# Products of gate and second-norm modulation chunks held back until the next weight chunk's low halves are in VectorE's program

## The chip, the cores and the metric

The kernel runs on one core of one Trainium2 chip. Its time is the device time of one execution in microseconds (us); lower is better. The core's engines run side by side, each through an instruction list of its own: TensorE (PE: matmuls, with PEld for its weight loads), VectorE (DVE), ScalarE (ACT), GpSimd (POOL) and SyncE (SP, which issues most of the transfers). Semaphores order them against each other.

## The reference, cut to what matters

One layer of a decoder for 256 tokens of width 2048. Attention (16 heads of sparse attention and 8 of retention) and an expert stage are each wrapped in a norm with modulation in front and a gated residual add behind:

```python
c_act = jax.nn.silu(c)
mod = (c_act @ w_ada[l] + b_ada[l]).reshape(B, 6, 1, D)
shift1, scale1, gate1, shift2, scale2, gate2 = jnp.moveaxis(mod, 1, 0)
h = rmsnorm(x, g_norm_mix[l]) * (1.0 + scale1) + shift1
q_a, k_c, ..., g_r = split_cols(h @ w_in[l], IN_SIZES)
...
x = x + gate1 * (jnp.concatenate([o_nsa, o_ret], axis=-1) @ w_out[l])
h2 = rmsnorm(x, g_norm_ffn[l]) * (1.0 + scale2) + shift2
x = x + gate2 * peer_ffn(h2, peer_w_q[l], peer_sub_keys[l], peer_u[l], peer_v[l])
```

The change touches the computation of `mod`: six vectors of 2048, each a product of a 2048 x 2048 part of `w_ada` with one vector.

## The kernel before

**Two stages.** Up to about 545 us come the modulation, the first norm, the input projection, both kinds of attention and the output projection (`woutN`). The expert stage follows, up to the end at 1855 us. Weights are read once, in chunks of 128 partitions x 2048 floats (1 MB).

**A weight chunk.** `load` issues its transfer on SP's queue into a tile `raw`; there are four such slots in the first stage. `split_to` makes two parts of it, each in two column halves: ScalarE rounds it to a high part `whi` (L157), and VectorE subtracts that from it to leave a low part `wlo` (L158). There are two slots of each. TensorE then does three products for each block (activation high x weight high, high x low, low x high), so that a chunk of the output projection is 24 matmuls of 512 columns (L453). The 16 chunks of `woutN` make four tiles of 512 output columns (q = 0 to 3, four chunks each, chunks 0 to 15). Behind each tile VectorE multiplies the sums by the row of gate1 (`xg`, L719) and adds the result to the residual `xT` (L720).

**A modulation chunk.** The modulation weights are 96 more chunks of the same size, `adaT[j, k]`: j is one of the six vectors, k one of 16 pieces of it. Each uses one of the same four raw slots. VectorE multiplies it by the row of silu(c) and sums along the row into one column of `modc` (L198, in place). It is named the product here. It frees the slot, and the next transfer into that slot waits on SP's queue for it, as it waits elsewhere for a low half (L158). The chunks are taken from the list `todo` in the order j = 1 and 0 mixed, then 2, 4, 3, and six of 5; `background(pace)` takes as many as the table `PACE` says after each weight chunk. The rest of j = 5 follows in the expert stage.

**The gate row.** When the last j = 2 chunk is done, TensorE transposes that column block of `modc` (psg1, L203), ScalarE copies it out (`row2t`, L204), GpSimd's queue stores it (L205) and loads it again as a 1 MB tile with the row in every partition (`g1`, L210). The `xg` multiplications read `g1`.

**Order.** A scheduler sets each engine's instruction order from the program order and priorities. `tc.keep_in_program_order` keeps an instruction at its place in the program. The retention heads run between the chunks of the last projection tiles; their scores are `scr` (L646, L647), which read query and key blocks that VectorE puts into `xT` (L430).

Of the kernel before, what the change touches and what calls it, by code (L numbers as in the profile page):

```python
# [17 lines left out]
OP = mybir.AluOpType  # L18
# [5 lines left out]
KB = D // P  # L24
# [7 lines left out]
LATE = 6  # L32
# [83 lines left out]
def body(ctx, tc, a, out, dbg=None, stop=None):  # L116
    nc = tc.nc
# [28 lines left out]
    def load(src):  # L146
        r = raw_tile()
        i = nc.sync.dma_start(r, src)
        if ring:
            tc.keep_in_program_order(i)  # L150
        return r

    def split_to(r, hi, lo, parts=1):
        n = hi.shape[-1] // parts
        for i in range(parts):
            sl = slice(i * n, i * n + n)
            nc.scalar.copy(hi[:, sl], r[:, sl])  # L157
            nc.vector.tensor_sub(lo[:, sl], r[:, sl], hi[:, sl].bitcast(F32))  # L158

    def split(r, n=2048, parts=2):  # L160
        hi, lo = chunk_tile("whi", F32R)[:, 0:n], chunk_tile("wlo", F32R)[:, 0:n]
        split_to(r[:, 0:n], hi, lo, parts)
        return hi, lo
# [8 lines left out]
    b_col = cols[:, 0:96].rearrange("p (j k) -> p j k", k=KB)  # L172
    g_mix, g_ffn = cols[:, 96:112], cols[:, 112:128]
# [3 lines left out]
    modc = base.tile([P, 6, KB], F32, name="modc")  # L177
    scol = base.tile([P, 2, KB], F32, name="scol")
    def c_row(pool, psum=None, dst=None):

        r = pool.tile([P, D], F32, name="crow") if dst is None else dst
        if psum is None:
            nc.sync.dma_start(r, bass.AP(tensor=a["c"].tensor, offset=a["c"].offset, ap=[[0, P], [1, D]]))
            nc.scalar.activation(r, r, AF.Silu)
            return r
        c1 = raw_tile()[0:1, :]
        nc.sync.dma_start(c1, a["c"])
        for q in range(4):
            sl = slice(q * 512, (q + 1) * 512)
            ps = psum.tile([P, 512], F32, name="psc_", tag="A")  # L190
            nc.tensor.matmul(ps, ones[0:1, :], c1[:, sl], start=True, stop=True)
            nc.scalar.activation(r[:, sl], ps, AF.Silu)
        return r

    def ada_chunk(j, k, crow):

        r = load(a["adaT"][j, k])
        nc.vector.scalar_tensor_tensor(r, r, 1.0, crow, op0=OP.mult, op1=OP.mult, accum_out=modc[:, j, k:k + 1])  # L198

    def gate_store(j, ps, ident, t):  # L200

        row = dram.tile([1, D], F32, name=f"row{j}")
        nc.tensor.transpose(ps, modc[:, j, :], ident)  # L203
        nc.scalar.copy(t, ps)  # L204
        nc.gpsimd.dma_start(row.rearrange("o (k p) -> (o k) p", p=P), t)  # L205
        return row

    def row_load(dst, row):

        nc.gpsimd.dma_start(dst, bass.AP(tensor=row.tensor, offset=row.offset, ap=[[0, P], [1, D]]))  # L210
# [30 lines left out]
    def t_block(pool, src_chunk, tag="A", **kw):  # L241
        return t_blocks(pool, [src_chunk], (tag,), **kw)[0]

    def summed(ps, dst, n=S):

        nc.scalar.copy(dst, ps[:, 1, 0:n])
        nc.vector.tensor_add(dst, dst, ps[:, 0, 0:n])
# [31 lines left out]
    with ExitStack() as fctx:  # L279
# [32 lines left out]
        crow = c_row(fp, pp)  # L312
# [15 lines left out]
        def background(n=1):  # L328
            credit[0] += PACE[n] if isinstance(n, str) else n
            n = int(credit[0] + 1e-6)  # L330
            credit[0] -= n
            for _ in range(n):
                if not todo:
                    return
                j, k = todo.pop(0)
                ada_chunk(j, k, crow)
                if j == 0:
                    nc.vector.tensor_add(modc[:, 0:2, k], modc[:, 0:2, k], b_col[:, 0:2, k])
                    nc.vector.tensor_scalar(scol[:, 0, k:k + 1], modc[:, 1, k:k + 1], 1.0, g_mix[:, k:k + 1],
                                            op0=OP.add, op1=OP.mult)  # L340
                elif 1 < j < 5 and k == KB - 1:
                    nc.vector.tensor_add(modc[:, j, :], modc[:, j, :], b_col[:, j, :])
                    if j == 4:
                        nc.vector.scalar_tensor_tensor(scol[:, 1, :], modc[:, 4, :], 1.0, g_ffn, op0=OP.add, op1=OP.mult)

        def win_row(src, k, n):
            r = raw_tile()
# [14 lines left out]
        def row_in(k):  # L362
            while len(todo) > 80 + LATE - 2 * (k + 1):
                background(1)
            modulate(k, k + 1, xT[:, k:k + 1, :], 0, 0, hh, hl)

        def wait_in(dst, bk):
            for i, b in enumerate(bk):
                if i % 2:
                    nc.vector.tensor_copy(dst[:, 2 * i:2 * i + 2, :], b)  # L370
                else:
                    nc.scalar.copy(dst[:, 2 * i:2 * i + 2, :], b)

        background(2)
        bk = banks("bkA", [P, 2, S], "AASSTTOO")
        for k in range(KH):
# [66 lines left out]
        def n_tile(i, src="winN", tag="A", pace="tile"):  # L443
            ps = [pp.tile([P, 512], F32, name="psN", tag=tag) for _ in range(2)]
            for c in range(4):
                hi, lo = split(load(a[src][i, c].rearrange("p k e -> p (k e)")))
                for kk in range(4):
                    k = 4 * c + kk
                    w = slice(kk * 512, (kk + 1) * 512)
                    for tt in range(2):  # L450
                        ts_ = slice(tt * P, (tt + 1) * P)
                        for j, (x, y) in enumerate(((hh, hi), (hh, lo), (hl, hi))):
                            nc.tensor.matmul(ps[tt], x[:, k, ts_], y[:, w], start=k == 0 and j == 0,  # L453
                                             stop=k == KB - 1 and j == 2)
                background(pace)
            return ps
# [19 lines left out]
        for kv in range(2):  # L476
# [9 lines left out]
            for pb in range(16):  # L486
                i = nc.tensor.matmul(psc, w1[:, pb * P:(pb + 1) * P], blk[:, pb], start=pb == 0, stop=pb == 15)
# [34 lines left out]
        for gp in range(2):  # L522
# [3 lines left out]
            for r in range(4):  # L526
# [5 lines left out]
                for hf in range(2):  # L532
# [5 lines left out]
                    for br in range(2):  # L538
# [6 lines left out]
                        for tt, sl in ((0, slice(0, 128)), (1, slice(128, 384))):  # L545
# [3 lines left out]
                                                 accum_out=den[:, hf, tt, br:br + 1])  # L549
# [14 lines left out]
                f = lambda x: x.rearrange("p a b c d -> p (a b c) d")  # L564
# [140 lines left out]
        for q in range(4):  # L705
            sl = slice(q * 512, (q + 1) * 512)
            ps = n_tile(q, "woutN", "AS"[q % 2], "out")
            if q == 0:
                while any(j == 2 for j, _ in todo):
                    background(1)  # L710
                g1 = fp.tile([P, D], F32, name="g1", tag="cT")
                row_load(g1, gate_store(2, pp.tile([P, P], F32, name="psg1", tag="T")[0:KB, :], ident,
                                        fp.tile([KB, P], F32, name="row2t")))
            if q == 3:
                background(len(todo))
            with tc.high_priority(offset=100 if q == 3 else 0):
                for tt in range(2):
                    t = fp.tile([P, 512], F32, name="xg", tag="tmp2", bufs=3)
                    nc.vector.tensor_mul(t, ps[tt], g1[:, sl])  # L719
                    nc.vector.tensor_add(x2[:, tt, sl], x2[:, tt, sl], t)  # L720
                    sq = fp.tile([P, 512], F32, name="sq2", tag="tmp2", bufs=3)
                    nc.scalar.activation(sq, x2[:, tt, sl], AF.Square, accum_out=ss[:, tt, q:q + 1])
                    nc.gpsimd.dma_start(x2d[:, tt, sl], x2[:, tt, sl])
# [23 lines left out]
    with ExitStack() as gctx:  # L747
# [49 lines left out]
        pin = tc.keep_in_program_order  # L797
# [76 lines left out]
        def rows_in(q):  # L874

            ps = up.tile([P, 512], F32, name="psh", tag=bank("S"))
            for i in range(4):
                nc.tensor.transpose(ps[0:NS, i * P:(i + 1) * P], xT[:, 4 * q + i, TD:S], ident)
            sl = slice(q * 512, (q + 1) * 512)
            nc.scalar.copy(h2t[0:NS, sl], ps[0:NS])  # L880
            nc.gpsimd.dma_start(h2t[NS:P, sl], h2t[0:NS, sl])
# [299 lines left out]
        crow2 = gp_.tile([P, D], F32, name="crow2", tag="X1")  # L1181
# [3 lines left out]
        for i in range(16):  # L1185
            ps = first[i] if i < 2 else t_block(up, wq(i), qbank(i), dst=early if i == 2 else None)
            q = tk.tile([P, S], F32, name="pq", bufs=3)
            summed(ps, q)
            pend.append((i, q))
            if i < KB - LATE:  # L1190
                ada_chunk(5, LATE + i, crow2)
            if 4 <= i < 8:
                rows_in(i - 4)
            if i > 1:
                scores(*pend.pop(0))
            if i == 10:
                cands(1, 0, 4)
            elif i in EARLY:
                pick(1, EARLY.index(i))
# [142 lines left out]
def build(tc, a, out, dbg=None):  # L1342
    with ExitStack() as ctx:
        body(ctx, tc, a, out, dbg)
# [17 lines left out]
```

## Time and profile before

| | us |
|---|---|
| median of 3 runs | 1858.06 (1857.24 to 1858.55) |
| profiled execution | 1856.91 |
| its span | 1855.2 |
| PE busy | 1793.1 (97%) |
| DVE busy | 1485.7 (80%) |
| ACT busy | 708.7 (38%) |
| POOL busy | 366.1 (20%) |
| products L198, 96 of 2283 ns | 219.0 |
| low halves L158, 174 of 1181 ns | 200.6 |
| high halves L157, 174 of 1018 ns | 168.5 |

The span is that of one profiled execution from its first to its last instruction. "Busy" is the time in which the engine had an instruction at work; how much of it sets the end is seen only from the waits. In the rows below, `out<-in` names what is written and read, `x2` is a count, and brackets hold the idle time ahead with what ended it.

### The profile page before, as it was taken

How to read it: one execution, taken by the hardware profiler on the slowest of the kernel's cores; microseconds unless marked ns; L12 is line 12 of the kernel's file. 1: busy time of each engine (PE TensorE's matmuls, PEld its weight loads, DVE VectorE, ACT ScalarE, POOL GpSimd, SP SyncE). 2: the span in 40 equal slices, each digit the busy share in tenths (PEclk: the TensorE clock that was granted, in tenths of full speed). 3: DMA queues.
4: the chain of work that ended last, by engine and by line, in shares of the span. 5: the costliest groups of instructions: out<-in, count | busy, mean ns of one | idle time of the engine just before them, and what ended most of it. 6: DMA issues, size and time to landing. Idle time of an engine off the chain costs nothing.

```text
span 1855.2 us, 28510 instructions
## 1 busy us (share of the span) xinstructions
PE 1793.1 (97%) x11264; PEld 1571.5 (85%) x11264; DVE 1485.7 (80%) x2336; ACT 708.7 (38%) x1284; POOL 366.1 (20%) x259
## 2 busy tenths in 40 slices
PE   5899999999889999999999999999999999999997
PEld 4899878797767899999997777779999998777775
DVE  7988889889779999586498999983555558998878
ACT  3444453745435421021045555541111114555554
POOL 1000001011010012211124434420111114544210
PEclk9999899999999999999999999999999999999999
DMA  8989887889887799999889999989999989999992
GB/s 341 409 320 362 313 308 292 342 302 334 318 338 279 278 322 364 424 366 376 332 346 386 423 420 416 409 355 425 367 345 359 354 316 404 426 421 403 388 316 99
DMA packets 94616, 653.96 MB, mean 353 GB/s; under 512 B 11409, under 2 KB 11633, under 8 KB 18449
## 3 DMA queue, kind: packets, MB, share of 16 engines
q1 hardware_dynamic: 66818, 467.78, 65.2%
q0 software_dynamic: 27664, 184.37, 25.3%
q8 instruction: 88, 1.44, 0.3%
q14 instruction: 46, 0.38, 0.1%
HBM read 644.97 MB, written 4.22 MB: 350 GB/s over the span
## 4 chain that ended last, share of the span: by engine, by line
PE 87%; DVE 7%; DMA 3%; issue 1%; ACT 1%; POOL 0%; SPq 0%; ACTq 0%; POOLq 0%; DVEq 0%
PE acc L990 31%; PE psU L1111 28%; PE psN L453 8%; PE psD L354 4%; PE psA L237 3%; PE bkB L354 2%; DMA raw<-in_adaT 2%; PE psA L238 1%; PE pg L1096 1%; DVE raw L198 1%; DVE wlo L158 1%; PE bkC L354 1%; PE bvB L406 1%; DMA raw<-in_winA 1%; PE pT L552 1%
## 5 line engine op out<-in xcount | busy, mean ns | idle before, releaser
L1111 PE MATMUL psU<-xT,raw 128*128 128x160 f32 x4096 | 569.5, 300 | 0.0
L1111 PEld LDWEIGHTS psU<-xT,raw 128*128 128x128 f32 x4096 | 558.3, 190 | 0.4
L990 PE MATMUL acc<-whi,cc 128*128 128x512 f32 x1512 | 369.1, 391 | 0.0
L990 PEld LDWEIGHTS acc<-whi,cc 128*128 128x128 f32 x1512 | 283.8, 188 | 70.0 <-issue 1.5
L967 DVE TENSOR_TENSOR wlo<-raw,whi 128x2048 fp32r<-128x2048 f32 x126 | 288.1, 2287 | 55.1 <-issue 47.4
L990 PE MATMUL acc<-wlo,cc 128*128 128x512 f32 x1008 | 254.2, 392 | 0.8 <-DVE wlo L967 0.6
L964 ACT CAST whi<-raw 128x2048 fp32r<-128x2048 f32 x126 | 240.7, 1911 | 0.5 <-DMA raw<-in_v 0.5
L198 DVE SCALAR_TENSOR_TENSOR raw<-raw,crow 128x2048 f32<-128x2048 f32 x96 | 219.0, 2283 | 19.7 <-DMA raw<-in_adaT 19.6
L157 ACT CAST whi<-raw 128x1024 fp32r<-128x1024 f32 (+1 forms) x174 | 168.5, 1018 | 167.1 <-DMA raw<-in_winA 32.4
L158 DVE TENSOR_TENSOR wlo<-raw,whi 128x1024 fp32r<-128x1024 f32 (+1 forms) x174 | 200.6, 1181 | 24.2 <-ACT whi L157 23.8
L990 PEld LDWEIGHTS acc<-wlo,cc 128*128 128x128 f32 x1008 | 161.5, 161 | 63.8 <-DVE wlo L967 3.1
L453 PE MATMUL psN<-whi,act 128*128 128x512 f32 x512 | 166.9, 402 | 1.4 <-ACT act L677 0.7
L1117 DVE TENSOR_TENSOR X<-X,ge 128x160 f32<-128x160 f32 (+19 forms) x94 | 25.8, 276 | 162.7 <-ACT ge L1116 160.5
L1113 ACT ACTIVATE X<-psU 128x160 f32<-128x160 f32 (+19 forms) x102 | 25.6, 251 | 315.6 <-PE psU L1111 299.6
L453 PEld LDWEIGHTS psN<-whi,act 128*128 128x128 f32 x512 | 95.9, 189 | 25.6 <-issue 1.7
L453 PE MATMUL psN<-wlo,act 128*128 128x512 f32 x256 | 103.3, 404 | 3.4 <-DVE wlo L158 3.4
L953 ACT CAST cc<-X 128x192 fp32r<-128x192 f32 x126 | 44.0, 352 | 148.1 <-PE acc L990 147.5
L237 PE MATMUL psA<-act,whi 128*128 128x512 f32 x240 | 87.2, 404 | 3.8 <-ACT whi L157 3.8
L806 POOL DMA_INDIRECT rows<-in_urow,sx x32 | 67.1, 2097 | 105.3 <-DVE rows L847 100.4
L806 POOL DMA_INDIRECT s<-in_urow,sx x26 | 53.9, 2072 | 120.6 <-DVE s L847 86.5
L354 PE MATMUL psD<-act,whi 128*128 128x256 f32 x384 | 75.4, 294 | 0.6 <-ACT whi L157 0.6
L969 ACT CAST cc<-cc 128x64 fp32r<-128x64 f32 x126 | 30.4, 243 | 117.2 <-DVE cc L954 117.2
(363 smaller groups left out, 2551.0 us busy)
## 6 DMA issues: line engine op xcount, KB each, us to landing
raw<-in_u SPq DMA_DIRECT2D x128, 1024.0 KB
raw<-in_v SPq DMA_DIRECT2D x128, 1024.0 KB
raw<-in_adaT SPq DMA_DIRECT2D x96, 1024.0 KB
raw<-in_winN SPq DMA_DIRECT2D x16, 1024.0 KB
raw<-in_woutN SPq DMA_DIRECT2D x16, 1024.0 KB
raw<-in_wqT SPq DMA_DIRECT2D x16, 1024.0 KB
raw<-in_winB SPq DMA_DIRECT2D x16, 832.0 KB
raw<-in_winD SPq DMA_DIRECT2D x12, 1024.0 KB
```

The costliest lines, as they stand in the source:

```text
L157: nc.scalar.copy(hi[:, sl], r[:, sl])
L158: nc.vector.tensor_sub(lo[:, sl], r[:, sl], hi[:, sl].bitcast(F32))
L198: nc.vector.scalar_tensor_tensor(r, r, 1.0, crow, op0=OP.mult, op1=OP.mult, accum_out=modc[:, j, k:k + 1])
L237: nc.tensor.matmul(p_, hi[:, sl], act[:, k], start=k == 0, stop=False, skip_group_check=True)
L354: nc.tensor.matmul(bank[:, b, :], x[:, w], y[:, k, :], start=k == k0 and n == 0 and first, stop=k == k1 - 1 and n == 2, skip_group_check=True)
L453: nc.tensor.matmul(ps[tt], x[:, k, ts_], y[:, w], start=k == 0 and j == 0, stop=k == KB - 1 and j == 2)
L806: pin(nc.gpsimd.indirect_dma_start(out=r, out_offset=None, in_=src, in_offset=bass.IndirectOffsetOnAxis(ap=o, axis=0)))
L953: inorder(nc.scalar.copy(ch, xb(j)))
L964: inorder(nc.scalar.copy(hi, r))
L967: nc.vector.tensor_sub(lo[:, i:i + n], r[:, i:i + n], hi[:, i:i + n].bitcast(F32))
L990: return nc.tensor.matmul(acc[c][0:m], x, w[:, c[1] * 512:(c[1] + 1) * 512], start=jj == 0 and n == 0, stop=jj == HALF - 1 and n == 2 - c[ ...
L1111: nc.tensor.matmul(ps, w[:, k * P:(k + 1) * P], xT[:, k, 0:TU], start=k == 0, stop=k == KB - 1)
```

## The change

`ada_chunk` now issues the transfer and returns the product as a function. For j = 0 and 1 (the first norm's shift and scale) it is called at once, as before; so it is for the chunks of j = 5 in the expert stage. For j = 2 to 5 of `background` it is put in the list `pend_ada`. `split_to` empties that list behind the low halves of the next weight chunk, with `keep_in_program_order`. A second waiting product, the gate row at q = 0 and the end of the list at q = 3 empty it through `settle` at their place, without it. The bias add of `modc` and the second norm's scale go along with the last product of their vector.

```diff
         for i in range(parts):
             sl = slice(i * n, i * n + n)
             nc.scalar.copy(hi[:, sl], r[:, sl])
             nc.vector.tensor_sub(lo[:, sl], r[:, sl], hi[:, sl].bitcast(F32))
+        while pend_ada:
+            pend_ada.pop(0)(tc.keep_in_program_order)
+
+    pend_ada = []
...
     def ada_chunk(j, k, crow):
         r = load(a["adaT"][j, k])
-        nc.vector.scalar_tensor_tensor(r, r, 1.0, crow, op0=OP.mult, op1=OP.mult, accum_out=modc[:, j, k:k + 1])
+
+        def f(pin=lambda i: i):
+            pin(nc.vector.scalar_tensor_tensor(r, r, 1.0, crow, op0=OP.mult, op1=OP.mult, accum_out=modc[:, j, k:k + 1]))
+        return f
...
-                ada_chunk(j, k, crow)
+                f = ada_chunk(j, k, crow)
                 if j == 0:
+                    f()
                     nc.vector.tensor_add(modc[:, 0:2, k], modc[:, 0:2, k], b_col[:, 0:2, k])
...
-                elif 1 < j < 5 and k == KB - 1:
-                    nc.vector.tensor_add(modc[:, j, :], modc[:, j, :], b_col[:, j, :])
-                    if j == 4:
-                        nc.vector.scalar_tensor_tensor(scol[:, 1, :], modc[:, 4, :], 1.0, g_ffn, op0=OP.add, op1=OP.mult)
+                elif j == 1:
+                    f()
+                else:
+                    settle()
+
+                    def rest(pin=lambda i: i, f=f, j=j, k=k):
+                        f(pin)
+                        if j < 5 and k == KB - 1:
+                            nc.vector.tensor_add(modc[:, j, :], modc[:, j, :], b_col[:, j, :])
+                            if j == 4:
+                                nc.vector.scalar_tensor_tensor(scol[:, 1, :], modc[:, 4, :], 1.0, g_ffn, op0=OP.add, op1=OP.mult)
+                    pend_ada.append(rest)
+
+        def settle():
+            while pend_ada:
+                pend_ada.pop(0)()
...
                 while any(j == 2 for j, _ in todo):
                     background(1)
+                settle()
...
             if q == 3:
                 background(len(todo))
+                settle()
...
-                ada_chunk(5, LATE + i, crow2)
+                ada_chunk(5, LATE + i, crow2)()
```

In the changed file the lines are shifted: the product is L204, `xg` L741, the add to `xT` L742, psg1 L210, a matmul of the output projection L473, the add before the scores L450.

Every engine's order changes between about 200 and 545 us; before and behind that it is the same. Three places follow. The numbers at the names tell tiles apart.

VectorE around chunks 5 to 7 of the output projection, before. The low halves `wlo_4480` are chunk 5, `wlo_4515` chunk 6, `wlo_4550` chunk 7; a row that writes `modc` is a product:

```order
L198 SCALAR_TENSOR_TENSOR raw_4544,modc_65<-raw_4544,crow_95 128x2048
L158 TENSOR_TENSOR wlo_4480<-raw_4477,whi_4479 128x1024 x2
L678 TENSOR_TENSOR act_70<-oT_90,act_70 128x256
L198 SCALAR_TENSOR_TENSOR raw_4625,modc_65<-raw_4625,crow_95 128x2048
L158 TENSOR_TENSOR wlo_4515<-raw_4512,whi_4514 128x1024 x2
L158 TENSOR_TENSOR wlo_4550<-raw_4547,whi_4549 128x1024
L719 TENSOR_TENSOR xg_4428<-psN_4281,g1_4420 128x512
L158 TENSOR_TENSOR wlo_4550<-raw_4547,whi_4549 128x1024
```

The same place now, with chunk 5 as `wlo_4479`, chunk 6 as `wlo_4514`, chunk 7 as `wlo_4549`:

```order
L158 TENSOR_TENSOR wlo_4479<-raw_4476,whi_4478 128x1024 x2
L204 SCALAR_TENSOR_TENSOR raw_4474,modc_65<-raw_4474,crow_95 128x2048
L741 TENSOR_TENSOR xg_4428<-psN_4280,g1_4420 128x512
L158 TENSOR_TENSOR wlo_4514<-raw_4511,whi_4513 128x1024 x2
L204 SCALAR_TENSOR_TENSOR raw_4509,modc_65<-raw_4509,crow_95 128x2048
L742 TENSOR_TENSOR xT_60<-xT_60,xg_4428 128x512
L741 TENSOR_TENSOR xg_4434<-psN_4281,g1_4420 128x512
L158 TENSOR_TENSOR wlo_4549<-raw_4546,whi_4548 128x1024
L742 TENSOR_TENSOR xT_60<-xT_60,xg_4434 128x512
L158 TENSOR_TENSOR wlo_4549<-raw_4546,whi_4548 128x1024
```

The product ahead of chunk 6 is now one that is three products earlier in the list, and the first `xg`, which reads `g1`, has moved from behind chunk 6 to ahead of it.

TensorE where chunk 5 begins, before. Chunk 3 is `whi_4390`, chunk 5 `whi_4479`; psT is a head's transpose:

```order
L516 MATMUL psT_4259<-small_79,orr_4073 128x128 x2
L203 MATMUL psg1_4421<-small_79,modc_65 16x128
L453 MATMUL psN_4281<-whi_4390,act_70 128x512
L453 MATMUL psN_4282<-whi_4390,act_70 128x512
L453 MATMUL psN_4440<-whi_4479,act_70 128x512
L453 MATMUL psN_4441<-whi_4479,act_70 128x512
L453 MATMUL psN_4281<-whi_4390,act_70 128x512
L453 MATMUL psN_4281<-wlo_4391,act_70 128x512
```

The same place now, with chunk 3 as `whi_4389`, chunk 4 as `whi_4444`, chunk 5 as `whi_4478`. Psg1 stands 20 rows of chunks 4 and 3 above the first matmul of chunk 4 that is shown here:

```order
L473 MATMUL psN_4280<-whi_4389,act_70 128x512
L473 MATMUL psN_4281<-whi_4389,act_70 128x512
L473 MATMUL psN_4281<-wlo_4390,act_70 128x512
L473 MATMUL psN_4281<-whi_4389,act_70 128x512
L473 MATMUL psN_4441<-wlo_4445,act_70 128x512
L473 MATMUL psN_4441<-whi_4444,act_70 128x512
L473 MATMUL psN_4440<-whi_4478,act_70 128x512
L473 MATMUL psN_4441<-whi_4478,act_70 128x512
```

Chunk 3 held one of the two `whi` slots until behind chunk 5 (6 of its matmuls stood among or after those of chunk 5); now it ends ahead of chunk 5, and chunk 5 takes the slot that chunk 3 leaves.

VectorE ahead of the last retention scores' query block (`xT_60<-cT_91`), before:

```order
L158 TENSOR_TENSOR wlo_4088<-raw_4085,whi_4087 128x1024
L672 TENSOR_TENSOR orr_3352<-orr_3352,sg_3560 128x256
L198 SCALAR_TENSOR_TENSOR raw_4152,modc_65<-raw_4152,crow_95 128x2048
L662 BN_AGGR bmv_3374<-bst_3373 128x2 x2
L661 BN_STATS bst_3398<-por_3394 128x6 x2
L649 TENSOR_TENSOR at_3974<-scr_3971,dec_3969 128x384
L198 SCALAR_TENSOR_TENSOR raw_4155,modc_65<-raw_4155,crow_95 128x2048
L430 TENSOR_TENSOR xT_60<-cT_91,psD_4002 128x512
```

The same place now:

```order
L158 TENSOR_TENSOR wlo_4087<-raw_4084,whi_4086 128x1024
L204 SCALAR_TENSOR_TENSOR raw_4054,modc_65<-raw_4054,crow_95 128x2048
L450 TENSOR_TENSOR xT_60<-cT_91,psD_4002 128x512
L683 TENSOR_SCALAR brs_3349<-bmv_3348 128x2
L692 TENSOR_TENSOR orr_3326<-orr_3326,sg_3559 128x256
```

Between the low halves of chunk 12 of the last input tiles (`winN`) and that add stood two products and several small steps; now one product stands there. On TensorE the scores that read it stand 13 matmuls later than before.

## Prediction

> **What bounds the kernel now.** I read the page first, then stretches of 20 us, then TensorE's waits in the stretch whose order changes, and last VectorE's, ScalarE's and GpSimd's rows around each wait.
>
> ```profile
> span 1855.2 us, 28510 instructions
> PE 1793.1 (97%) x11264; PEld 1571.5 (85%) x11264; DVE 1485.7 (80%) x2336; ACT 708.7 (38%) x1284; POOL 366.1 (20%) x259
> L198 DVE SCALAR_TENSOR_TENSOR raw<-raw,crow 128x2048 f32<-128x2048 f32 x96 | 219.0, 2283 | 19.7 <-DMA raw<-in_adaT 19.6
> ```
>
> The profiled execution took 1856.91 us: the span and 1.7 us around it. That is 1.15 us below the median of the runs. TensorE (PE) is busy in 97% of the span, so the change can win only what TensorE loses in the stretch that it reorders (about 200 to 545 us; later every engine's order is as before). A product (L198) costs 2.28 us of VectorE, and before the 96 of them VectorE stood 19.6 us waiting for their transfers. Those 19.6 us are no forecast of the gain: VectorE's idle time counts only where TensorE then waits.
>
> ```profile
> 400.00:420.00 20.00, 20.00 (x162) 19.58 (x161) 18.03 (x27) 8.87 (x15) 5.55 (x3) 1.00 0.88 312
> 420.00:440.00 20.00, 18.08 (x87) 14.61 (x87) 18.40 (x32) 9.81 (x16) 2.69 (x2) 1.00 0.97 348
> 440.00:460.00 20.00, 20.00 (x95) 16.09 (x93) 19.08 (x37) 13.32 (x19) 3.79 (x3) 1.00 0.91 351
> 460.00:480.00 20.00, 19.28 (x87) 15.20 (x87) 15.47 (x21) 8.18 (x16) 1.26 (x2) 1.00 0.85 309
> 480.00:500.00 20.00, 15.92 (x61) 12.16 (x60) 14.41 (x16) 7.23 (x10) 1.66 (x3) 0.91 0.84 303
> 500.00:520.00 20.00, 20.00 (x88) 16.05 (x87) 15.58 (x16) 9.24 (x12) 1.08 (x2) 1.00 0.82 303
> 540.00:560.00 20.00, 12.57 (x54) 8.95 (x52) 14.78 (x36) 9.60 (x27) 4.01 (x6) 0.81 0.79 295
> 200.00:420.00 220.00, 218.86 (x1411) 188.16 (x1411) 193.62 (x396) 112.94 (x250) 22.33 (x24) 0.98 0.84 314
> ```
>
> The columns are the stretch, its length, busy time of PE, PEld, DVE, ACT and POOL, granted clock, DMA share, GB/s. From 200 to 420 us TensorE misses 1.1 us in all. It misses 1.92 in 420:440, 0.72 in 460:480 and 4.08 in 480:500. What is missing from 544 us on is the passage into the second norm, where the order stays. The waits have these causes (us in total, times, longest):
>
> ```profile
> PE psN L453 <- DVE wlo L158: 3.4, 1, 3.4
> PE scr L646 <- DVE xT L430: 1.9, 1, 1.9
> PE psN L453 <- ACT act L677: 0.7, 1, 0.7
> PE psN L453 <- ACT whi L157: 0.7, 1, 0.7
> 482.00:484.00 2.00, 1.33 (x6) 0.69 (x5) 0.00 (x0) 1.50 (x2) 0.00 (x0) 1.00 0.84 348
> 484.00:487.75 3.75, 0.33 (x3) 0.00 (x1) 3.50 (x4) 2.38 (x3) 0.00 (x0) 0.99 0.51 151
> 487.75:491.00 3.25, 3.25 (x8) 2.57 (x9) 3.25 (x4) 0.00 (x0) 0.00 (x0) 0.50 0.82 325
> 491.00:495.00 4.00, 4.00 (x19) 3.22 (x18) 3.33 (x5) 0.99 (x3) 1.10 (x2) 0.99 1.02 383
> ```
>
> The wait of 3.42 us before 487.75 is followed by 3.25 us at a granted clock of 0.50: 1.6 us more. The wait of 1.92 us is not (clock 1.00 in 420:440).
>
> **The change, part by part.** No instruction is added or removed on TensorE, VectorE or the queues; the change is all order.
>
> *The removed wait at 484.* Chunks are those of the output projection, 0 to 15. VectorE's rows of before:
>
> ```profile
> 417.60 2.29 DVE L198 SCALAR_TENSOR_TENSOR raw<-raw,crow 128x2048 f32<-128x2048 f32 x1 [1.97 <-DMA raw<-in_adaT]
> 420.82 2.28 DVE L198 SCALAR_TENSOR_TENSOR raw<-raw,crow 128x2048 f32<-128x2048 f32 x1
> 423.02 0.68 DVE L430 TENSOR_TENSOR xT<-cT,psD 128x512 f32<-128x512 f32 x1
> 475.38 2.36 DVE L158 TENSOR_TENSOR wlo<-raw,whi 128x1024 fp32r<-128x1024 f32 x2
> 484.25 2.29 DVE L198 SCALAR_TENSOR_TENSOR raw<-raw,crow 128x2048 f32<-128x2048 f32 x1 [6.18 <-DMA raw<-in_adaT]
> 486.47 3.49 DVE L158 TENSOR_TENSOR wlo<-raw,whi 128x1024 fp32r<-128x1024 f32 x3
> 477.77 6.39 DMA raw<-in_adaT
> 468.20 4.87 DMA raw<-in_adaT
> 409.70 7.81 DMA raw<-in_adaT
> ```
>
> Chunk 5's low halves free a raw slot at 477.7, a product's transfer starts into it and lands 6.39 us later, and the product stands in VectorE's program ahead of chunk 6's low halves, which TensorE needs. In the new order chunk 6's low halves stand ahead of the product that follows them, and each product's transfer is issued at least a whole chunk before its turn. So 3.42 + 1.6 = 5.0 us go. The last three rows, from the chain of waits, show what a 1 MB transfer takes from issue: 4.87 to 7.81 us.
>
> *The removed wait at 421.* Two products (one late by 1.97) stand before the add at 423.02 for which the scores wait. In the new order one product stands between the low halves before and that add, and on TensorE the scores come 13 matmuls (13 x 0.234 = 3.0 us) later. So 1.92 go; kept in full if that one product's transfer is 3 us late, so 0 to 1.92.
>
> *The small waits at 475 and 483.* 0.72 is for the head's output behind a 2.00 us cast on ScalarE (first row below). The new order casts chunk 5 after the heads, so this goes. The 0.67 goes into the next term.
>
> **What is late next.** I count from P, the gate transpose psg1 on TensorE (474.22 before).
>
> ```profile
> 473.26 2.00 ACT L157 CAST whi<-raw 128x1024 fp32r<-128x1024 f32 x2 [4.59 <-PE psN L453]
> 474.22 0.27 PE L203 MATMUL psg<-small,modc 128*16 128x128 f32 x1
> 475.53 0.24 ACT L204 COPY row2t<-psg 16x128 f32<-16x128 f32 x1
> 476.06 0.55 POOL L205 DMA_DIRECT2D row<-row2t  x1 [10.27 <-ACT row2t L204]
> 480.81 0.56 POOL L210 DMA_DIRECT2D g<-row  x1 [4.21 <-DMA row<-row2t]
> 464.66 1.06 ACT whi L157
> 465.74 1.23 DVE wlo L158
> 517.09 2.00 ACT L157 CAST whi<-raw 128x1024 fp32r<-128x1024 f32 x2 [3.55 <-PE psN L453]
> 522.69 2.00 ACT L157 CAST whi<-raw 128x1024 fp32r<-128x1024 f32 x2 [3.60 <-PE psN L453]
> 545.12 0.69 DVE L720 TENSOR_TENSOR xT<-xT,xg 128x512 f32<-128x512 f32 x1
> 538.70 2.29 DVE L198 SCALAR_TENSOR_TENSOR raw<-raw,crow 128x2048 f32<-128x2048 f32 x1
> 544.39 0.69 DVE L719 TENSOR_TENSOR xg<-psN,g 128x512 f32<-128x512 f32 x1 [3.39 <-PE psN L453]
> ```
>
> *Chunk 5's cast.* Two casts wait for TensorE and start 5.60 us apart: a chunk has 24 matmuls, so one is 0.234 us. After psg1 the new order has 8 matmuls of chunk 4, 12 of chunk 3, 2 of chunk 4, then chunk 5. Chunk 5's cast waits for the buffer that chunk 3 holds: P + 20 x 0.234 = P + 4.7. From the start of a cast to the first low half is 2.31 us (464.66 to 465.74 + 1.23). TensorE has 4 matmuls (0.94) to fill it: a wait of 1.4 us, against the 0.67 of before.
>
> *The gate row ahead of chunk 6.* In the new order the first multiplication by the gate row, xg, stands ahead of chunk 6's low halves on VectorE (before, behind them). The copy no longer queues behind a cast: P + 0.3. The store follows 0.53 us later, the load 4.75 after it: issued at P + 5.6. It lands after 4.87 to 7.81 us (the transfers above); I take 6.39, since other loads are in flight then too: P + 12.0. xg 0.69 and half a lo pair 1.15: chunk 6's first low half at P + 13.8. TensorE comes to it at P + 4.7 + 2.3 + 22 x 0.234 + 2 x 0.234 = P + 12.6. A wait of 1.2 us; by the ends of the landing time 0 (then the product ahead sets P + 12.3) to 2.6.
>
> *Chunk 7.* Behind it VectorE has the other half 1.15, a product 2.28, an add and a multiplication 1.37, chunk 7's half 1.15: P + 19.8. TensorE needs it after 24 matmuls, P + 19.4: 0.4 us, 0 to 1. At chunk 8 the same sum gives TensorE P + 25.4 and VectorE P + 25.1: no wait.
>
> The matmuls after a wait run at half clock only where the idle time reaches some bound between 1.92 and 3.42. The Trainium skill, "TensorE: Matmul & The Clock Gate", Part 1, puts it at an idle window of about 3.4 us, after which the clock is halved until about 3.4 us of work; the trace agrees (3.42 idle, 3.25 at 0.50). By that rule the new waits, all under 3.4, cost only themselves. Were the bound at 2 us, chunk 6 at its late end would cost 1.6 more.
>
> *The end.* Before, one product (538.70) stands behind the last low halves, and VectorE then idles 3.39 until TensorE ends at 544.39. Now three stand there: 2.28 x 3 = 6.8 us ahead of the last xg. The last chunk's cast at about 533.9 (two steps of 5.6 after 522.69) gives both low halves by 537.4, so the products end at 544.2: no delay if their transfers are there, up to 1.6 if the last one, issued at about 535.3, takes 8.4. I take 0.3.
>
> *The weights.* A weight chunk's raw slot is freed by the low halves two chunks earlier, or by the product behind them. A cast starts when the chunk two before is used up; the low halves of that one were done 11.2 - 3.5 = 7.7 us earlier, or 5.4 with a product between. TensorE bears a cast 3.3 us late (5.6 less 2.3). So a load has 11.0 or 8.7 us, and takes 4.87 to 7.81. Covered while VectorE keeps up; I take 0.6 for the places where it doesn't (chunks 7 and 8 behind the gate row, and a few chunks of the projections), 0 to 9.
>
> The sum: 5.0 + 1.9 + 0.7 + 0.7 = 8.3 us go; 1.4 + 1.2 + 0.4 + 0.3 + 0.6 = 3.9 us come. Net -4.4: 1852.5 for a profiled execution, 1853.6 on the median.
>
> **The rivals.**
> 1. *A late gate row takes the wait's place.* GpSimd's queue shares the engines with the weight loads; landing at its late end gives 2.6 instead of 1.2 at chunk 6, and chunk 8's load, which hangs on chunk 6's low halves, costs another 1: the gain falls by 2.4 to 2.0, 1856.1. For it: the load is on VectorE's path now. Against: of the weight loads only chunk 7's is issued between P + 6 and P + 12. The Trainium skill, "DMA: Bandwidth & Descriptors", Queues, rings and completion order, says that each engine takes turns between queues packet by packet, which speaks for the late end; no row here isolates it.
> 2. *The weights come late: slower.* VectorE is busy 18.0, 18.4 and 19.1 of 20 us in the three stretches from 400 to 460. Where it falls more than about 1 us behind TensorE, a load of 7.8 us misses 8.7, and the next slot is freed later still. At 1.5 us each it takes three such chunks (4.4 us) to cancel the gain and six to lose: -4.4 + 9 = +4.6, 1862.7. For it: the loads start about one chunk later than before all along. Against: with products never waiting, VectorE falls behind less.
> 3. *The change only moves the waits.* The scores at 421 wait for another late product, and the waits around the last heads keep their sum: 3.4 + 1.6 + 1.9 give way to equal ones, 1858.
>
> **How the numbers follow.** The forecast's case (3.7 to 8.4 us gained) has 0.53; rival 1 (0 to 3.7 gained) 0.19; rival 3 0.11; rival 2 0.17. Within 0.2% (3.7 us), about what a measurement can tell from no change, lie rivals 1 and 3: 0.30. Bounds: all old waits gone and none new is 1858.06 - 8.4 = 1849.7; upward it takes in most of rival 2. The range is 1849.3 to 1861.0; the forecast's own is 1849.7 to 1854.4.
>
> **What would show it.** Right: no VectorE wait for an adaT transfer over 1 us from 420 to 530; 420:440 full for TensorE; two or three waits of TensorE of 0.5 to 2 us between 470 and 495, and a granted clock near 1.00 in 480:500 there; xg ahead of chunk 6 ended by the gate row's transfer. Wrong: waits of ScalarE's casts for weight transfers (winN, woutN), a half clock anywhere in 200 to 540, or a wait over 3 us before chunk 6.

## The result: slower, and the profile after

The changed kernel takes 1872.82 us (median of 4 runs, 1870.55 to 1875.74) against 1858.30 for the kernel before: 1.0068 times as long, with a 95% interval of 1.0048 to 1.0087. The profiled executions show the same difference: the span goes from 1855.2 to 1869.3 us, 14.1 us more.

Where it comes from, in the two traces: the last matmul of the output projection starts at 554.29 us instead of 544.66 (+9.6); the first transpose of the second norm at 562.34 instead of 549.81 (+12.5, so 2.9 in the passage); the first matmul of the expert scan at 676.13 instead of 662.01 (+14.1, so 1.6 in the loop between). Behind that nothing is added. Of the 1.6 us, about 1.2 are the clock: at the loop's start TensorE works for 6.62 us at a granted clock of 0.50 (569.8 to 580.1 us), before for 4.15 us at 0.51 (559.3 to 566.2).

Stretches of 20 us of the changed kernel, with the columns as in the prediction:

```profile
300.00:320.00 20.00, 18.41 (x133) 17.07 (x132) 18.95 (x24) 7.26 (x8) 2.94 (x1) 1.00 0.77 286
420.00:440.00 20.00, 17.27 (x78) 13.62 (x77) 17.52 (x29) 10.60 (x18) 2.74 (x3) 0.92 0.80 291
440.00:460.00 20.00, 14.59 (x62) 11.49 (x61) 18.91 (x38) 11.23 (x18) 2.13 (x3) 0.84 0.96 354
480.00:500.00 20.00, 18.81 (x82) 14.48 (x81) 11.96 (x14) 5.81 (x9) 1.12 (x2) 1.00 0.74 262
500.00:520.00 20.00, 19.12 (x81) 14.62 (x80) 15.50 (x17) 10.06 (x16) 2.17 (x4) 1.00 0.94 356
520.00:540.00 20.00, 19.80 (x85) 15.63 (x84) 18.16 (x19) 7.80 (x12) 1.08 (x2) 1.00 0.97 354
```

480:500 is as forecast: the wait of 3.4 us is gone and the clock stays at 1.00. But 300:320, which was full, misses 1.6 us, 420:440 misses 2.7 at a clock of 0.92, and 440:460, which was full, misses 5.4 at 0.84.

What ScalarE's casts (`whi`) and VectorE's products mostly waited for between 200 us and the end of the output projection (total, times, longest), first before, then after:

```profile
ACT whi L157 <- PE psN L453: 32.1, 10, 6.4
ACT whi L157 <- issue: 20.6, 8, 4.0
ACT whi L157 <- PE psD L354: 16.7, 7, 5.1
DVE raw L198 <- DMA raw<-in_adaT: 16.2, 9, 6.2
```

```profile
ACT whi L157 <- DMA raw<-in_woutN: 40.3, 11, 8.2
ACT whi L157 <- DMA raw<-in_winN: 28.3, 8, 7.3
ACT whi L157 <- PE psN L473: 17.5, 7, 4.4
ACT whi L157 <- DMA raw<-in_winD: 3.3, 2, 2.0
DVE raw L204 <- DMA raw<-in_adaT: 4.1, 2, 2.4
```

These rows hold the main result. Before, no cast in this stretch is seen to wait for a weight transfer: it waited for TensorE to give up a `whi` slot, and by then the weights were there. (`issue` means that the profile names no releaser. Four of these eight casts start at 494.73, 500.33, 505.93 and 511.53 us, 5.60 apart, which is TensorE's pace.) After, casts wait 72 us for weight transfers. The products' own waits fell from 16.2 to 4.1 us, which is what the change does, and which was worth little.

The longest new stall, from VectorE's, SP's, ScalarE's and TensorE's rows:

```profile
443.44 2.28 DVE L204 SCALAR_TENSOR_TENSOR raw<-raw,crow 128x2048 f32<-128x2048 f32 x1
445.76 0.33 SPq L148 DMA_DIRECT2D raw<-in_woutN  x1
452.52 1.99 ACT L157 CAST whi<-raw 128x1024 fp32r<-128x1024 f32 x2 [1.59 <-DMA raw<-in_woutN]
454.53 1.28 ACT L653 ACT_TABLE_LOAD   x1
456.48 0.79 PE L473 MATMUL psN<-whi,act 128*128 128x512 f32 x1 [3.23 <-ACT sg L653]
```

A product that stands behind the low halves frees its slot at 445.7; the load of chunk 1 of the output projection goes out at 445.76 and lands after 6.7 us; the cast waits for it, and behind the cast on ScalarE stands the retention gate, for which TensorE waits 3.23 us.

**How long a slot is held.** Transfers and products come in the same order, so each product can be matched with its transfer: the time from issue to the start of the product, mean of those issued in the stretch (their count).

| kernel | 200 to 420 us | 420 to 540 us |
|---|---|---|
| before | 9.1 (36) | 6.8 (15) |
| changed | 13.9 (34) | 15.4 (15) |

A modulation chunk holds one of the four slots 5 to 9 us longer, and weights have to come through the same slots.

**The passage.** VectorE's last two products and xg, and TensorE's last matmul and first transpose:

```profile
552.50 2.29 DVE L204 SCALAR_TENSOR_TENSOR raw<-raw,crow 128x2048 f32<-128x2048 f32 x1
554.71 2.29 DVE L204 SCALAR_TENSOR_TENSOR raw<-raw,crow 128x2048 f32<-128x2048 f32 x1
556.92 0.69 DVE L741 TENSOR_TENSOR xg<-psN,g 128x512 f32<-128x512 f32 x1
554.29 0.39 PE L473 MATMUL psN<-whi,act 128*128 128x512 f32 x1
562.34 0.87 PE L758 MATMUL psX<-small,xn 128*128 128x128 f32 x3 [7.66 <-DVE xn L753]
```

TensorE is done at 554.7, xg starts 2.2 us later, behind three products in a row (the first from 550.29).

### The profile page after: what moved, and what is told of

Its sections match the earlier page's. It is cut to its first block, busy times and chain, and to the rows that moved or that the text cites. A ratio compares the mean times of both kernels' runs of the same rounds, so it can differ in the third digit from the quotient of the medians.

```text
span 1869.3 us, 28493 instructions
## 1 busy us (share of the span) xinstructions
PE 1798.3 (96%) x11264; PEld 1574.0 (84%) x11264; DVE 1486.0 (79%) x2336; ACT 707.6 (38%) x1282; POOL 357.7 (19%) x259
## 4 chain that ended last, share of the span: by engine, by line
PE 81%; DVE 11%; DMA 5%; issue 2%; ACT 1%; POOL 0%; SPq 0%; ACTq 0%; POOLq 0%; DVEq 0%
PE acc L1012 30%; PE psU L1133 28%; PE psN L473 5%; PE psA L244 3%; DVE raw L204 2%; DVE wlo L158 2%; PE bkB L374 2%; DMA raw<-in_woutN 2%; PE psD L374 2%; PE psA L245 1%; PE pg L1118 1%; PE bkC L374 1%; PE bvB L426 1%; DMA raw<-in_winN 1%; DMA raw<-in_winA 1%
## 5 line engine op out<-in xcount | busy, mean ns | idle before, releaser
L157 ACT CAST whi<-raw 128x1024 fp32r<-128x1024 f32 (+1 forms) x174 | 168.6, 1019 | 198.8 <-DMA raw<-in_woutN 40.3
L204 DVE SCALAR_TENSOR_TENSOR raw<-raw,crow 128x2048 f32<-128x2048 f32 x96 | 218.9, 2284 | 6.5 <-DMA raw<-in_adaT 6.5
L473 PE MATMUL psN<-whi,act 128*128 128x512 f32 x512 | 169.4, 406 | 7.9 <-ACT whi L157 4.7
L473 PEld LDWEIGHTS psN<-whi,act 128*128 128x128 f32 x512 | 96.8, 191 | 33.1 <-ACT whi L157 6.5
L473 PE MATMUL psN<-wlo,act 128*128 128x512 f32 x256 | 104.6, 408 | 2.5 <-DVE wlo L158 2.5
L828 POOL DMA_INDIRECT rows<-in_v,sx x25 | 59.1, 2366 | 80.3 <-DVE sp L875 56.7
```

Of the source, the lines that this page charges most:

```text
L204: pin(nc.vector.scalar_tensor_tensor(r, r, 1.0, crow, op0=OP.mult, op1=OP.mult, accum_out=modc[:, j, k:k + 1]))
L828: pin(nc.gpsimd.indirect_dma_start(out=r, out_offset=None, in_=src, in_offset=bass.IndirectOffsetOnAxis(ap=o, axis=0)))
```

## The experiments

Theory S: a modulation chunk keeps its raw slot until the product at its pinned place, so weight loads go out late; the loss lies where the lead was least. The rivals are named in the texts. Without `keep_in_program_order`, the later place in the program leaves every engine's order as it was before, row for row: the pin is the whole change.

### Where: the two halves

The products are held back only ahead of the output projection:

```diff
+        defer = [True]
...
+                elif not defer[0]:
+                    settle()
+                    f()
...
+        defer[0] = False   # ahead of the loop over the output projection's tiles
```

> The products are held back only in the projections ahead of the output projection; inside the output projection they are given at once, as before. Theory S (a raw slot is given back a product later, so weight loads start late, worst between 300 and 455 us): this half carries most of the loss, the stalls at 315 (1.7), 433 (1.9), 449 to 453 (6.1 and the half clock behind) all stay: +7 to +11 us against before. Theory E (the loss is at the end and in the output projection, from the three products ahead of the last xg and the pinned low halves of chunks 5 to 15): this half costs little, 0 to +3 us.

Measured: 1869.21 against 1860.12, 1.0045 (1.0028 to 1.0061). The stalls at 315 (1.5), 433 (1.3) and 449 to 451 (1.3 and 3.7) stay, and TensorE's wait in the passage is 4.8 us as before. Theory S; E falls.

The same with `False` ahead and `True` in the output projection:

> The products are held back only inside the output projection; ahead of it the order is that of before, row for row. Theory S: the wait at 421 (2.1) stays, the one at 484 (5.0 with the half clock) goes, chunks 5 to 15 cost about 3, the end 2 to 3, the expert stage's first loop 1 to 2: 0 to +4 us against before. Theory E: +10 us or more.

Measured: 1859.14 against 1860.12, 0.9996 (0.9984 to 1.0009). The wait at 484 with its half clock is gone; 1.4 and 0.5 us at chunk 5 and 1.0 at the last chunk are new, and the output projection ends at 543.8 instead of 545.0. TensorE's wait in the passage is 7.6 us instead of 4.8, and the gain is gone again. So the hold ahead of the output projection makes the loss, and the hold inside it gives back at its end what it wins.

### A queue or a slot

```diff
-                nc.sync.dma_start(x2[:, tt, q * 512:(q + 1) * 512], a["x"][...])
+                nc.gpsimd.dma_start(x2[:, tt, q * 512:(q + 1) * 512], a["x"][...])
```

> The changed kernel with the eight 512-column loads of x into xT issued on GpSimd's queue instead of SP's. Theory Q (the load of the last input chunk but one stands on SP's queue behind an x load, which waits 5.4 us for the last scores; the stalls of 433 to 453 follow from it): that load is issued 3 to 5 us earlier and the kernel is 4 to 8 us faster than the changed one. Theory S: the slot itself comes free late, so 0 to 2 us faster.

Measured: 1874.13 against 1860.12, 1.0068 (1.0047 to 1.009), the changed kernel's ratio. SP's row:

```profile
428.90 0.33 SPq L148 DMA_DIRECT2D raw<-in_winN  x1
```

In the changed kernel this load goes out at 426.95, behind the x load; here, with the x loads off the queue, at 428.90, in a profile in which the last matmul of the tiles `psD`, which end just ahead of this, starts 2.1 us later (419.26 against 417.17). Counted from there it goes out at 9.6 us instead of 9.8: it did not move. Theory Q falls: the slot was not free earlier.

### The end

```diff
-LATE = 6
+LATE = 4
```

> The changed kernel with two fewer products in the first stage (four of the last vector instead of six; the two move into the expert stage's first loop). If the three products ahead of the last xg set the passage into the second norm, xg starts at TensorE's end and the passage is 2.2 us shorter; the two products and loads cost 0 to 4.6 us in the next loop, where VectorE is nearly full. All in all -2 to +2 us against the changed kernel.

Measured: 1873.78 against 1860.12, 1.0079 (1.0058 to 1.0099). TensorE's wait in the passage:

```profile
PE psX L758 <- DVE xn L753: 4.8, 1, 4.8
```

The wait is 4.8 us, as before, and the first transpose comes at 559.39 instead of 562.34. So the 2.9 us of the passage are the products ahead of the last xg. But the loop behind takes 103.3 us instead of 102.0, and the time as a whole is no better: the two products only moved.

### One slot more

There is no room for a fifth slot, so four kernels with smaller attention buffers make the comparison:

```diff
-dict(raw=4, whi=2, wlo=2)
+dict(raw=5, whi=2, wlo=2)
...
-nal = fp.tile([P, 384], F32, name="nal", bufs=4)
+nal = fp.tile([P, 384], F32, name="nal", bufs=2)
...   (pTs and tmp2 3 to 2; hid, msn, bst, bmv 2 to 1)
```

Four slots, not held back:

> The kernel before with smaller attention buffers (two instead of four tiles nal, two instead of three of pTs and tmp2, one instead of two of four tiny ones), which make room for a fifth raw slot that is not used here. It is the base of the next three: 0 to +10 us against before, all of it ahead of 420 us.

Four slots, held back:

> The changed kernel with the same smaller attention buffers and four raw slots: by every theory +9 to +16 us against the base.

Five slots, not held back:

> The kernel before with the smaller attention buffers and five raw slots. Theory S (weight loads are late because a slot comes free a product later): before had lead to spare, so 0 to -4 us against the base.

Five slots, held back:

> The changed kernel with the smaller attention buffers and five raw slots. Theory S: the fifth slot gives back the chunk of lead, casts no longer wait for winN and woutN transfers (68 us with four slots), and only the end's 2 to 3 us and the 1 to 2 us of the next loop stay: 0 to +5 us against five slots without the holding back. Theory O (the new order of VectorE and TensorE costs the time itself, by low halves and attention steps standing behind products): +9 to +16 us as with four slots.

| | not held back | held back |
|---|---|---|
| four slots | 1867.86 (1.0029, 1.0018 to 1.0040) | 1878.85 (1.0085, 1.0067 to 1.0103) |
| five slots | 1874.41 (1.0061, 1.0039 to 1.0084) | 1865.19 (1.0015, 1.0005 to 1.0025) |

(Medians, and ratios to the kernel before, 1862.13.) With four slots the hold costs 11.0 us, with five it gains 9.2. The casts' waits for weights, four slots and then five, both held back:

```profile
ACT whi L157 <- DMA raw<-in_woutN: 40.9, 10, 8.1
ACT whi L157 <- DMA raw<-in_winN: 22.4, 5, 5.9
ACT whi L157 <- DMA raw<-in_winD: 17.7, 3, 10.5
```

```profile
ACT whi L157 <- DMA raw<-in_woutN: 9.7, 2, 5.4
ACT whi L157 <- DMA raw<-in_winD: 8.9, 2, 5.2
ACT whi L157 <- DMA raw<-in_winN: 8.5, 3, 5.8
```

81 us become 27, though the products hold their slots even longer with five (17.2 and 18.8 us in the two stretches of the table above, against 14.2 and 15.3). Without the hold these waits are 17 us with four slots and 5 with five. (The profiled execution with four slots, held back, was its slowest: 1885.16 us, the others 1878.50 to 1878.99.)

Both expectations for five slots were missed. Without the hold, five slots made the kernel 6.6 us slower, not faster: its trace shows a wait of 6.7 us of TensorE on an attention step of VectorE at 442 which four slots don't show. So its base is a bad one, and the 9.2 us, outside theory S's 0 to +5, are in part that. Each new set of buffers is also a new order, and all differences here hold that too. What stands clear of the bad base: held back, the fifth slot gains 13.7 us (1878.85 to 1865.19), and this kernel is also 2.7 us faster than the one with four slots and no hold. Theory O, that the hold costs +9 to +16 whatever the slots, falls.

### Place and pin

All products pinned, but directly behind the low halves of the weight chunk ahead:

```diff
-                    pend_ada.append(rest)
+                    rest(tc.keep_in_program_order)
```

> All products of the changed kernel are kept in program order, but at their own place, directly behind the low halves of the weight chunk ahead, not behind those of the next: pinned, and not held back. Theory S: the raw slots come free a chunk earlier, so casts wait little for winN and woutN transfers (under 25 us instead of 69), while VectorE waits for adaT transfers (over 12 us instead of 4); -3 to +5 us against before. Theory P (pinning itself, whatever the place, makes the bad order): +9 us or more, as the changed kernel.

Measured: 1875.39 against 1859.31, 1.0086 (1.0068 to 1.0105). By the time alone this is theory P. The casts' waits:

```profile
ACT whi L157 <- DMA raw<-in_winN: 21.9, 6, 7.2
ACT whi L157 <- DMA raw<-in_winD: 17.4, 4, 7.2
ACT whi L157 <- DMA raw<-in_woutN: 4.4, 2, 2.5
```

Both expected sizes were missed: 26 us for winN and woutN, not under 25, and no wait of VectorE for adaT at all. But the two halves differ: ahead of the output projection the products hold their slots for 16.1 us, longer than in the changed kernel (13.9), and all the loss is there; in the output projection they hold them for 10.9 us (15.4), casts wait 4.4 us (40.3), and TensorE loses nothing between 474 us and the end of the output projection. This suggests that pinning is harmless where weight chunks follow each other every 5.6 us, and costs where attention stands between them, since the product then waits in its slot for the low halves ahead of it.

So the pin at this place, in the output projection alone (the diff above, with `defer` as in the second kernel):

> The products are pinned directly behind the low halves of the weight chunk ahead, in the output projection only; ahead of it the order is that of before. Theory S (what costs is the time for which a product keeps its slot): the products keep their slots for 10 to 11 us there, as in the kernel that pins them so everywhere, casts wait under 10 us for woutN transfers, nothing is lost between 475 and the end of the output projection but 1 to 2 us at chunk 5, and the passage is 4.9 us: -4 to -7 us against before. Theory P (pinning itself costs): 0 to +5 us.

Measured: 1855.71 against 1861.17, 0.9965 (0.9953 to 0.9977): 5.5 us faster than before, and the largest gain here. Its stretches from 480 on:

```profile
480.00:500.00 20.00, 19.56 (x84) 15.39 (x84) 17.83 (x19) 8.62 (x12) 1.66 (x3) 1.00 0.93 354
500.00:520.00 20.00, 20.00 (x87) 16.06 (x86) 16.62 (x18) 7.85 (x11) 1.08 (x2) 1.00 0.99 387
520.00:540.00 20.00, 20.00 (x87) 16.04 (x86) 17.30 (x18) 6.84 (x10) 1.08 (x2) 1.00 0.89 334
```

TensorE loses 0.4 us there, the products hold their slots for 10.2 us, and the wait in the passage is 5.4. Casts waited 20.9 us for woutN transfers, more than the 10 expected, but TensorE hardly waited for them (0.44 us at chunk 5). So theory S holds in the output projection, and P falls there. Ahead of it no run separates the pinned order from the long hold; that the fifth slot gains 13.7 us speaks for the hold.

### Smaller holds

Held back in the first three tiles of the output projection only (`defer[0] = q < 3`):

> The products are held back only in the first three tiles of the output projection; ahead of it and in its last tile they are given at once. The hold in the whole output projection took the wait at 484 away (its output projection ended 1 us earlier than before's) but left three products ahead of the last xg, a passage of 7.8 us instead of 4.9. Theory: without the hold in the last tile the passage is 4.9 to 5.5 us again: -2 to -5 us against before. If the passage stays at 7 us or over, the products ahead of the last xg are not set by the hold: 0 +- 2 us.

Measured: 1855.49 against 1859.31, 0.9979 (0.9965 to 0.9993). The gain came, but not as expected: the wait in the passage is 6.8 us, with one product ahead of the first xg and one behind it. And the wait at 421 is not in this trace, although every engine's order is that of before up to 442 us (there it was 1.92, in the kernel with the hold in the whole output projection 1.86). So that wait comes and goes between executions of one order, and what the gain is made of is not shown.

One product held back:

> Only one of the 96 products is held back behind the next low halves: the one whose transfer was 6.2 us late and stood ahead of chunk 6 (the 15th of the fourth vector). Theory S: one product costs the weight loads little, and the wait of 3.4 us and the half clock behind it go: -2 to -5 us against before. If any pinned product makes a wait of the same size elsewhere: 0 +- 2 us.

Measured: 1858.88, 1.0001 (0.9988 to 1.0014). The wait of 3.4 is gone, and one of 2.6 us before 511 us is there instead: another late product (its transfer 1.85 us behind VectorE) stands ahead of other low halves.

Three held back:

> That product and the two ahead of the last scores' query block (fifth and sixth of the same vector) are held back. Theory S: the two stand where weight loads had the least lead (the last input chunks), so the wait of 1.9 at 421 is exchanged for waits for weight transfers behind it: -4 to +3 us against before, and casts waiting for winN transfers between 415 and 450.

Measured: 1857.64, 0.999 (0.9976 to 1.0004). The wait of 1.9 at 421 is gone (which one trace does not prove, as just said), one of 1.8 at 438 is new, and casts wait 4.8 us for winN transfers, as theory S has it, though too few to lose by it.

The last one joins two of these products to the pin in the output projection:

> The same, and the two products that stood ahead of the last scores' query block are held back behind the next low halves. The wait of 2 us at 421 goes; by theory S two products that keep their slots some 6 us longer there give casts that wait for winN transfers behind 425: -3 to +3 us against the version without this.

Measured: 1857.45 against 1861.17, 0.9981 (0.9971 to 0.9991), no better than without: the wait of 1.8 at 424 is exchanged for one of 2.0 at 441, with no cast that waits for a winN transfer. That the stretch has no lead to spare for two products is not shown.

## Why the prediction was wrong

**The step that failed is "The weights"**: 0.6 us, with 0 to 9 as its range. The term says that the transfers of weights stay covered. They did not: casts wait 72 us for them instead of 0. Between 315 and 457 us of the changed kernel's trace TensorE waits 4.6 us for casts and low halves, 3.2 more behind a late cast (the stall at 456) and 2.2 around the heads, and two stretches at half clock cost 3.4. The kernel that holds back only ahead of the output projection is 9.1 us slower, and held back, a fifth slot gains 13.7 us and takes 54 of 81 us off the casts' waits. Three things were wrong in the term.

First, the lead was worked out where casts follow each other every 5.6 us, in the output projection, and taken over with a word ("a few chunks") for the projections ahead, where it was needed. There products wait behind low halves that wait for casts. The chain of waits of the changed kernel where the loss arises, with steps left out at the dots:

```profile
411.22 2.21 DVE raw L204 x2
413.47 7.65 DMA raw<-in_winN
421.22 1.05 ACT whi L157
...
426.95 6.97 DMA raw<-in_winN
433.94 1.05 ACT whi L157
...
443.53 2.22 DVE raw L204 x2
445.76 6.68 DMA raw<-in_woutN
```

A product frees a slot, a weight transfer takes 6.7 to 7.7 us, and the cast and TensorE wait for it: these are the stalls at 421, 433 and 453.

Second, the 3.3 us for which TensorE bears a late cast were counted for every load. They can be used once: a late cast makes late low halves, these free the slot late, and the next load starts late. In the output projection the chain of the changed kernel runs round this loop:

```profile
494.13 6.32 DMA raw<-in_woutN
500.55 1.06 ACT whi L157
501.63 1.23 DVE wlo L158
503.45 1.15 DVE wlo L158
504.62 7.65 DMA raw<-in_woutN
...
539.19 7.63 DMA raw<-in_woutN
```

Load, cast, low halves, sometimes a product, load: from chunk 7 to chunk 15 it takes 539.19 - 494.13 = 45.1 us, 5.63 a chunk, TensorE's own pace of 5.6. Before, the chain of this stretch was TensorE alone. So here the loop just keeps pace and costs little (waits of 0.52, 0.36, 0.20 and 0.25 us), but the reserve is used up. That the same happens ahead of the output projection is argued from the chain shown first.

Third, the rival had the mechanism, but its price (six chunks at 1.5 us) was of the same stretch, and had no half clock in it; it said 1862.7, and even that lay above the range (up to 1861.0).

**The waits that went.** The one at 484 with its half clock went, as forecast, and so did the scores' wait at 421; the kernel with the hold in the output projection alone shows the first by itself. That the second went by the change is not shown, since it is also absent from a trace with the order of before (above); the 1.9 us rested on one execution. In the changed kernel waits of 0.8 and 1.7 us for casts stand at 421 and 433 instead.

**Chunk 5's cast**: 1.4 forecast, 0.67 and 0.53 measured at 488 to 491. Right.

**The gate row** (1.2 and 0.4): wrong, it was never late. VectorE's xg starts at 494.02 without idle time. The wait of 0.5 at chunk 7 is for a weight transfer.

**The end**: 0.3 forecast, 2.2 measured from TensorE's end to xg, 2.9 with all of the passage. The three products were counted rightly; the last low halves were put 7.0 us ahead of TensorE's end (537.4 to 544.4), and with a late last load they came 4.3 ahead.

**Rival 1** (the gate row) did not happen; **rival 3** (the waits only move) is what the kernel with one held product did.

**The clock.** "The new waits, all under 3.4, cost only themselves" was wrong too, and so was a bound on the idle time between 1.92 and 3.42: a wait of 1.86 us was followed by half clock, and one of 2.65 was not (below).

## What to carry to other kernels

A wait that is taken away by running an instruction later has its price in everything that this instruction holds: here a slot that the next loads need. Count how long each user keeps a slot, in the trace and in the new order, and multiply by the users before counting the wait as won. And a reserve that a loop carries from one turn to the next can be spent once, not once a turn; where the place is right (here directly behind the low halves of the chunk ahead, and only where chunks follow each other closely) the same pin gains. And a wait that stands in one trace may be missing from the next with the same order: look at a second before counting it.

## What the hardware showed

Stretches around short waits of TensorE: three of the changed kernel, two of the kernel with the hold in the output projection alone, two of the kernel with one product held back:

```profile
433.10:436.50 3.40, 1.43 (x8) 0.87 (x7) 1.48 (x3) 2.56 (x4) 0.00 (x0) 1.00 1.02 426
436.50:439.60 3.10, 3.10 (x9) 2.37 (x9) 3.10 (x4) 1.50 (x3) 0.00 (x0) 0.53 0.50 114
456.50:460.30 3.80, 3.80 (x9) 3.02 (x10) 3.04 (x6) 2.23 (x6) 0.71 (x1) 0.50 0.99 377
421.90:425.30 3.40, 1.53 (x8) 1.26 (x8) 3.40 (x8) 0.19 (x1) 0.07 (x1) 1.00 0.98 337
425.30:428.70 3.40, 3.40 (x9) 2.67 (x9) 1.28 (x2) 0.62 (x1) 1.58 (x1) 0.51 1.01 392
508.50:511.35 2.85, 0.20 (x2) 0.00 (x1) 2.85 (x5) 0.29 (x1) 0.00 (x0) 1.00 0.96 364
511.35:514.80 3.45, 3.45 (x15) 2.81 (x16) 3.45 (x5) 2.33 (x4) 0.54 (x1) 1.00 0.85 309
```

The longest wait in 433.1 to 436.5 is 1.66 us, and a second of 0.30 follows it; TensorE was idle for 1.97 of 3.40 us. The 3.1 us behind it have a granted clock of 0.53. But it is not that two waits stand close together: in the second kernel a single wait of 1.86 us is followed by 3.4 us at 0.51, where before the same wait in the same order (1.92) left the clock at 1.00. Nor is it the length alone: in the third kernel a wait of 2.65 us is followed by 1.00. So waits well under 3.4 us can halve the clock in one execution and not in another, and what decides is not settled here. The two half-clock stretches of the changed kernel cost 1.5 and 1.9 us. The Trainium skill, "TensorE: Matmul & The Clock Gate", Part 1, names an idle window of about 3.4 us as what halves the clock; the first row and the fourth differ, with TensorE busy for 1.43 and 1.53 us in their 3.40.
